# Retention values by token, retention gates kept in SBUF, and their units spread among the merge gates' in a one-core streaming layer on Trainium2

## The chip, the cores and the metric

The kernel runs on one core of one Trainium2 chip. The engines are PE (TensorE, matrix products; PEld is its weight load, which overlaps), DVE (VectorE), ACT (ScalarE), POOL (GpSimd, which here only issues stores) and SP (SyncE, which issues loads). Each works through its own queue in order and waits on semaphores for the others. The metric is the device time of one launch in microseconds (us), the median of several runs; lower is better.

## The reference, cut to what matters

One layer of a hybrid encoder for 512 prompt tokens and 8 x 16 sample tokens, so five token tiles of 128 (T = 640 columns). All is float32. The part that the change touches is the retention mixer, four heads with keys of 128 and values of 256:

```
h = rms_norm(x, norm_mix_g)
z = h @ w_in_mix                       # split into rq, rk, rv, rg, fq, fk, fv, ff, zg
q = rotary(rq); k = rotary(rk) * 128 ** -0.5; v = rv
per chunk: inter = (q @ state) * inter_decay
           intra = ((q @ k.T) * intra_decay) @ v
           state = state * chunk_decay + (k * kv_decay).T @ v
o_ret = rms_norm(inter + intra).reshape(B, S, 1024) * silu(rg)   # norm over the 256 values of a head
br_ret = o_ret @ w_br_ret
g = sigmoid(zg)                        # two merge gates of 1024 columns
y = (g[0] * br_ret + g[1] * br_fox) @ w_out
```

Two SwiGLU half steps, the forgetting attention (FoX) and a per-layer embedding stand around it and are not touched.

## The kernel before, in words

**Products.** Activations lie with channels on the partitions and tokens along the free axis. Each large matrix product is made of float32r pieces: ACT casts a weight block to `wh` (L281), DVE makes the rest `wl` (L282), and three matmuls of 320 columns are run per pair of blocks. Units of kind "s" of the mixer's projection use `MixSeven`, a Strassen-like scheme of seven products: `after(i)` combines the PSUM banks behind product i on ACT (L815 to L820) and DVE (L816 to L834). DVE's L830 and L833 are the last readers of the banks of a unit, and PE's next products need those banks. Behind them the two finished tiles of 128 x 640 (`z0`, `z1`) are stored by POOL to DRAM (`zdram`, 320 KB each; L831, L834).

**Order.** `run_units` is a generator over a list of units (`units`): it loads raw weights two units ahead on SP, splits them, runs products and yields. The attention and retention work is written by hand beside it: each step of a retention head is followed by `fill(FILL_R)`, which advances the generator by 2.45 us of PE work by a clock of the kernel's own. `until(("rg", hd))` would advance it until a head's gates exist. From this the framework's scheduler makes one fixed order for each engine, so a step that becomes shorter or longer moves what stands behind it by some instructions.

**List of units before.** FoX units, values `rv`, then "s" units of two tiles each: 2 for `rq`, 2 for `rk`, 4 for the retention gates `rg` (one per head), 8 for the merge gates, then two embedding units and four units of the FoX branch (`w_br_fox`). The heads run while the merge gates' units and those behind them are fed. The last merge unit also carries `embed_begin` and `fox_fetch`.

**A retention head.** `flip` turns the keys, `scores` makes `at` (scores times decay, keys on the partitions), `states_p` the running prompt states `behind`. `values(dvb)` makes, for each half of the value channels, a PSUM bank of 128 value channels x 512 prompt tokens out of seven float32 products of 128 columns, and ACT copies it to `o` (L1405). `square` squares both halves on ACT (L1421, L1423) and adds them on DVE (L1424). `values_s` makes the sample tile with tokens on the partitions and sums its squares on ACT with an accumulator (L1416, L1417). `sizes` sums the prompt's squares over the partitions with four matmuls of one column (out `pa`, in `ones`, `blk`), gathers them (L1431, L1432), and runs `rsqrt_mean` on DVE (L338 to L345: a chain of small operations); L1434 scales the sample tile. `gates` loads the head's two gate tiles back from `zdram` on SP and puts Silu on them (ACT, L1452). `states` makes the sample states and updates them with four DVE operations (L1478), which POOL stores. `finish` multiplies the gates on (L1463), spreads the token factors over the partitions with four matmuls (out `pa`, in `sm`, `ty`), multiplies with them (L1464), turns the sample tile with two transposes (L227) and gates it (L1465); POOL stores both tiles to `retd`, from where the `w_br_ret` products read them.

Silu (L1452) and the Sigmoid of the FoX branch (L1534) use different ACT function tables; a change between them shows as ACT_TABLE_LOAD.

Of the kernel before, what the change touches and what calls it, by code (L numbers as in the profile page):

```python
# [14 lines left out]
ALU = mybir.AluOpType  # L15
# [4 lines left out]
P = 128  # L20
# [25 lines left out]

FILL_P0, FILL_P1, FILL_S0, FILL_S, FILL_R, FILL_B = 1.76, 1.6, 19.8, 10.0, 2.45, 6.4
# [83 lines left out]
def kernel(  # L131
# [667 lines left out]

    class MixSeven(Seven):  # L800
# [9 lines left out]
        def after(self, i):  # L810
            a, b, c = (self.banks[k][:, :H2] if k in self.banks else None for k in "abc")
            r0, r1 = (mix_norm.rb[:, sl] for sl in HALVES)
            if i == 1:
                s1, self.w1 = tmp(), tmp()
                nc.scalar.copy(s1, a)  # L815
                nc.vector.tensor_tensor(b, b, s1, op=ALU.subtract)  # L816
                nc.scalar.copy(self.w1, b)
            elif i == 2:
                self.z1 = blk()
                nc.scalar.copy(self.z1[:, H2:], c)  # L820
                nc.vector.tensor_tensor(c, c, self.w1, op=ALU.subtract)
            elif i == 3:
                self.z0 = blk()
                nc.vector.tensor_tensor(self.z0[:, :H2], a, r0, op=ALU.mult)
            elif i == 4:
                s5 = self.z1[:, H2:]
                nc.vector.tensor_tensor(s5, b, s5, op=ALU.subtract)
                nc.vector.tensor_tensor(s5, s5, r1, op=ALU.mult)
            elif i == 5:
                nc.vector.tensor_tensor(self.z0[:, H2:], c, r1, op=ALU.mult)  # L830
                nc.gpsimd.dma_start(zdram[self.n0], self.z0)  # L831
            elif i == 6:
                nc.vector.tensor_tensor(self.z1[:, :H2], b, r0, op=ALU.mult)  # L833
                nc.gpsimd.dma_start(zdram[self.n0 + 1], self.z1)  # L834
# [489 lines left out]
    class Retention:  # L1324
# [70 lines left out]
        def values(self, dvb):  # L1395
            if dvb == 0:
                self.o = []
            dsl = slice(dvb * P, (dvb + 1) * P)
            po = bank()
            for t in range(4):  # L1400
                mm(po[:, t * P:(t + 1) * P], self.vs[t][:, dsl], self.at[:, t, :], True, t == 0, skip_group_check=True)
                if t > 0:
                    mm(po[:, t * P:(t + 1) * P], self.behind[t - 1][:, dsl], self.qd[:, t - 1, :], False, True, skip_group_check=True)
            o = blk()
            nc.scalar.copy(o[:, :S], po)  # L1405
            self.o.append(o)

        def values_s(self):
# [6 lines left out]
            self.os, sq, self.ms = tmp([P, DV]), tmp([P, DV]), tiny(1)  # L1415
            nc.scalar.copy(self.os, po[:, :DV])  # L1416
            nc.scalar.activation(sq, self.os, AF.Square, accum_out=self.ms)  # L1417

        def square(self):
            self.sq = blk([P, S])  # L1420
            nc.scalar.activation(self.sq, self.o[0][:, :S], AF.Square)  # L1421
            sq = blk([P, S])
            nc.scalar.activation(sq, self.o[1][:, :S], AF.Square)  # L1423
            nc.vector.tensor_tensor(self.sq, self.sq, sq, op=ALU.add)  # L1424

        def sizes(self):
            pm = bank()
            for t in range(4):
                mm(pm[:, t:t + 1], self.sq[:, t * P:(t + 1) * P], ones[:, 0:1], True, True)
            sums = tiny(TB)  # L1430
            nc.vector.tensor_copy(sums[:, :4], pm[:, :4])  # L1431
            nc.vector.tensor_copy(sums[:, 4:], self.ms)  # L1432
            self.ro = rsqrt_mean(sums, TB, 1.0 / DV)
            nc.vector.tensor_scalar(self.os, self.os, self.ro[:, 4:], None, op0=ALU.mult)  # L1434
# [12 lines left out]
        def gates(self):  # L1447
            self.g = []
            for dvb in range(2):
                g = blk()  # L1450
                load(g, zdram[Z_RG + 2 * self.hd + dvb])
                nc.scalar.activation(g, g, AF.Silu)  # L1452
                self.g.append(g)

        def finish(self):
            s0, pt = bank(), bank()
            for t in range(4):
                mm(s0[:, t * P:(t + 1) * P], self.ro[:, t:t + 1].to_broadcast([P, P]), ident, True, True)
# [113 lines left out]
    units += units_s(Z_G1, O_ZG + D, 8) + units_s(Z_G0, O_ZG, 8)  # L1572
    units[-1].begin, units[-1].middle = embed_begin, fox_fetch
# [69 lines left out]
    for hd, r in enumerate(heads):  # L1643
        for step in (
# [3 lines left out]
            lambda: r.values(0), lambda: (r.values(1), r.square()), lambda: r.values_s(),  # L1648
# [134 lines left out]
```

## Time and profile before

| what | value |
| --- | --- |
| median of 3 runs | 1646.37 us (1645.69 to 1647.33) |
| profiled execution: own time / span | 1648.36 us / 1646.6 us |
| PE busy, share of the span | 1631.5 us, 99% |
| DVE, ACT, POOL busy | 1165.6 us, 734.6 us, 98.9 us |
| granted TensorE clock, mean | 0.999 |
| retention heads in the trace | from about 880 to 1045 us |
| DMA | 248.15 MB, mean 151 GB/s |

The profile is that of one execution. Its time from launch to end is 1648.36 us, the span from the first to the last instruction 1646.6 us. The rows below carry, for each piece of work, its start in us from the start of the span, its length, the engine, the line and the operation with output and input names (buffer numbers left out); a bracket gives the idle time just before it on its engine and what ended it.

### The profile page before, as it was taken

The numbers are of one execution on the slowest core, as the hardware profiler recorded it, in microseconds if no ns is written. First come the engines' busy times: TensorE is split into PE (matmuls) and PEld (weight loads), VectorE is DVE, ScalarE is ACT, GpSimd is POOL, SyncE is SP. The second block draws the span as 40 slices with busy tenths as digits, with TensorE's granted clock in tenths as the row PEclk, the third lists the DMA queues.
The fourth block names the chain that finished last, engine by engine and source line by source line (L and its number), as shares of the span: only waits on it lengthen the run. The fifth ranks groups of instructions, "written<-read, shape, count | busy, mean of one in ns | idle before, by whom it ended". The sixth has DMA issues, their size and how long they took to land.

```text
span 1646.6 us, 30526 instructions
## 1 busy us (share of the span) xinstructions
PE 1631.5 (99%) x12067; PEld 1562.8 (95%) x12067; DVE 1165.6 (71%) x2476; ACT 734.6 (45%) x1516; POOL 98.9 (6%) x180
## 2 busy tenths in 40 slices
PE   9999999999999999999999899999999999999999
PEld 8999999999999888888799898999999999999998
DVE  7884786586876646766688895658885678568663
ACT  7552354244455444444434345435553355235432
POOL 0000000000111111000001111001000000000000
PEclk9999999999999999999999999999999999999999
DMA  7244223423623235566775576634333424432531
GB/s 245 77 143 141 93 87 124 150 85 108 210 81 117 90 111 170 219 257 229 279 255 195 194 262 242 228 109 161 95 116 134 134 77 132 136 117 88 172 120 46
DMA packets 207360, 248.15 MB, mean 151 GB/s; under 512 B 10432, under 2 KB 176240, under 8 KB 203120
## 3 DMA queue, kind: packets, MB, share of 16 engines
q1 hardware_dynamic: 194976, 202.69, 37.5%
q0 software_dynamic: 12032, 43.42, 6.7%
q8 instruction: 95, 1.56, 0.4%
q14 instruction: 49, 0.40, 0.1%
q10 hardware_dynamic: 208, 0.08, 0.0%
HBM read 197.51 MB, written 48.65 MB: 149 GB/s over the span
## 4 chain that ended last, share of the span: by engine, by line
PE 92%; DVE 3%; DMA 3%; ACT 1%; issue 1%; SPq 0%; DVEq 0%; ACTq 0%
PE pa L204 70%; PE pg L204 18%; PE pa L227 4%; DMA raw<-in_ffn_w_in_dram 2%; DVE wl L282 1%; DMA kv<-zdram 1%; DMA blk<-zdram 0%; ACT tmp L532 0%; ACT wh L281 0%; PE pg L227 0%; DVE raw L433 0%; DMA kv<-in_x_prompt_dram 0%; ACT blk L281 0%; ACT L1452 0%; DVE raw L422 0%
## 5 line engine op out<-in xcount | busy, mean ns | idle before, releaser
L281 ACT CAST wh<-raw 128x512 fp32r<-128x512 f32 (+1 forms) x525 | 315.5, 613 | 501.7 <-PE pa L204 319.7
L204 PE MATMUL pa<-blk,wh 128*128 128x320 f32 x2344 | 509.7, 310 | 2.8 <-ACT wh L281 1.0
L282 DVE TENSOR_TENSOR wl<-raw,wh 128x512 fp32r<-128x512 f32 (+1 forms) x525 | 351.4, 678 | 98.9 <-ACT wh L281 95.3
L204 PEld LDWEIGHTS pa<-blk,wh 128*128 128x128 f32 x2344 | 386.3, 188 | 10.9 <-ACT wh L281 2.8
L204 PE MATMUL pa<-blk,wl 128*128 128x320 f32 x1172 | 343.0, 308 | 0.0
L204 PE MATMUL pa<-kv,wh 128*128 128x320 f32 x1344 | 251.6, 308 | 0.0
L204 PEld LDWEIGHTS pa<-blk,wl 128*128 128x128 f32 x1172 | 215.4, 188 | 0.0
L204 PEld LDWEIGHTS pa<-kv,wh 128*128 128x128 f32 x1344 | 210.6, 188 | 0.0
L204 PE MATMUL pg<-blk,wh 128*128 128x320 f32 x768 | 177.0, 317 | 5.1 <-DVE blk L833 2.7
L204 PE MATMUL pa<-blk,blk 128*128 128x320 f32 (+2 forms) x1064 | 168.7, 304 | 0.0
L204 PE MATMUL pa<-kv,wl 128*128 128x320 f32 x672 | 154.5, 308 | 0.0
L204 PEld LDWEIGHTS pa<-blk,blk 128*128 128x128 f32 (+1 forms) x1064 | 151.9, 183 | 1.9 <-PE pa L204 1.2
L204 PE MATMUL pg<-wh,blk 128*128 128x256 f32 x768 | 148.0, 286 | 0.0
L204 PEld LDWEIGHTS pg<-blk,wh 128*128 128x128 f32 x768 | 127.4, 189 | 12.0 <-issue 5.8
L204 PEld LDWEIGHTS pg<-wh,blk 128*128 128x128 f32 x768 | 120.8, 188 | 6.8 <-issue 5.2
L204 PE MATMUL pg<-blk,wl 128*128 128x320 f32 x384 | 119.1, 310 | 0.0
L204 PEld LDWEIGHTS pa<-kv,wl 128*128 128x128 f32 x672 | 112.7, 188 | 0.0
L204 PE MATMUL pg<-wl,blk 128*128 128x256 f32 x384 | 108.4, 283 | 0.0
L282 DVE TENSOR_TENSOR blk<-raw,blk 128x512 fp32r<-128x512 f32 x82 | 56.2, 688 | 41.5 <-ACT blk L281 29.7
L204 PE MATMUL pa<-wh,blk 128*128 128x256 f32 (+1 forms) x432 | 82.3, 285 | 0.0
L281 ACT CAST blk<-raw 128x512 fp32r<-128x512 f32 x82 | 50.6, 621 | 61.1 <-DMA raw<-in_ffn_w_in_dram 47.8
L204 PEld LDWEIGHTS pg<-wl,blk 128*128 128x128 f32 x384 | 72.2, 188 | 1.6 <-issue 1.1
(293 smaller groups left out, 2250.1 us busy)
## 6 DMA issues: line engine op xcount, KB each, us to landing
raw<-in_ffn_w_in_dram SPq DMA_DIRECT2D x86, 512.0 KB, 4.7
raw<-in_w_in_mix_dram SPq DMA_DIRECT2D x25, 1024.0 KB, 5.7
raw<-in_ffn_w_out_dram SPq DMA_DIRECT2D x16, 1024.0 KB, 5.1
kv<-in_cache_fox_k_dram SPq DMA_DIRECT2D x16, 1024.0 KB, 6.3
kv<-in_cache_fox_v_dram SPq DMA_DIRECT2D x16, 1024.0 KB, 6.5
blk<-xd SPq DMA_DIRECT2D x48, 320.0 KB, 5.4
xd<-blk POOLq DMA_DIRECT2D x40, 320.0 KB, 2.4
zdram<-blk POOLq DMA_DIRECT2D x32, 320.0 KB, 3.4
```

What stands on the lines that cost most here:

```text
L204: i = nc.tensor.matmul(out, lhsT, rhs, start=start, stop=stop, **kw)
L227: tick(nc.tensor.transpose(out, in_, ident[: in_.shape[0], : in_.shape[0]]), 0.11)
L281: nc.scalar.copy(hi, src)
L282: nc.vector.tensor_tensor(lo, src, hi, op=ALU.subtract)
```

## The change

It has four parts.

1. **Values by token.** `values(u)` now makes two token tiles (128 tokens x 256 value channels) per bank: the scores or the scaled queries are the stationary operand and the values the moving one, so seven float32 products of 256 columns per head stand for fourteen of 128. ACT copies the bank (L1414) and squares each token tile with an accumulator (L1416), so that the sums of squares stand per token where `rsqrt_mean` needs them. The one-column matmuls, `square` and the gathering copies are gone.
2. **Scaling by token, then transposes.** `sizes` scales all five token tiles on DVE (L1434, 128 x 256 each). `finish` turns them with ten transposes (L228), and DVE multiplies the gates directly with the transposed bank (L1460) and the sample part (L1461). The four spreading matmuls and one 128 x 512 multiplication per half are gone.
3. **Gates kept.** The units of `rg` leave their tiles in SBUF (`kept`); their eight stores to and eight loads from `zdram` are gone.
4. **Order of units.** Five merge units come ahead of the first `rg` unit, one each ahead of the second and the third, none ahead of the fourth, and the last one behind it.

```diff
+MERGE_THEN = 5, 1, 1, 0
...
             elif i == 5:
                 nc.vector.tensor_tensor(self.z0[:, H2:], c, r1, op=ALU.mult)
-                nc.gpsimd.dma_start(zdram[self.n0], self.z0)
+                self.out(self.n0, self.z0)
...
+        def out(self, n, z):
+            if Z_RG <= n < Z_G1:
+                kept[n] = z
+            else:
+                nc.gpsimd.dma_start(zdram[n], z)
...
-        def values(self, dvb):
-            if dvb == 0:
-                self.o = []
-            dsl = slice(dvb * P, (dvb + 1) * P)
-            po = bank()
-            for t in range(4):
-                mm(po[:, t * P:(t + 1) * P], self.vs[t][:, dsl], self.at[:, t, :], True, t == 0, skip_group_check=True)
+        def values(self, u):
+
+            if u == 0:
+                self.o, self.ms = [], tiny(TB)
+            po, o, sq = bank(), att(shape=(P, 2, DV)), tmp([P, DV])
+            for n in range(2):
+                t, out = 2 * u + n, po[:, n * DV:(n + 1) * DV]
+                mm(out, self.at[:, t, :], self.vs[t], True, t == 0, skip_group_check=True)
                 if t > 0:
-                    mm(po[:, t * P:(t + 1) * P], self.behind[t - 1][:, dsl], self.qd[:, t - 1, :], False, True, skip_group_check=True)
-            o = blk()
-            nc.scalar.copy(o[:, :S], po)
-            self.o.append(o)
+                    mm(out, self.qd[:, t - 1, :], self.behind[t - 1], False, True, skip_group_check=True)
+            nc.scalar.copy(o.rearrange("p n v -> p (n v)"), po)
+            for n in range(2):
+                nc.scalar.activation(sq, o[:, n, :], AF.Square, accum_out=self.ms[:, 2 * u + n:2 * u + n + 1])
+                self.o.append(o[:, n, :])
...
         def sizes(self):
-            pm = bank()
-            for t in range(4):
-                mm(pm[:, t:t + 1], self.sq[:, t * P:(t + 1) * P], ones[:, 0:1], True, True)
...
+            ro = rsqrt_mean(self.ms, TB, 1.0 / DV)
+            for t, o in enumerate(self.o):
+                nc.vector.tensor_scalar(o, o, ro[:, t:t + 1], None, op0=ALU.mult)
...
-                g = blk()
-                load(g, zdram[Z_RG + 2 * self.hd + dvb])
+                g = kept.pop(Z_RG + 2 * self.hd + dvb)
                 nc.scalar.activation(g, g, AF.Silu)
...
         def finish(self):
-            s0, pt = bank(), bank()
-            for t in range(4):
-                mm(s0[:, t * P:(t + 1) * P], self.ro[:, t:t + 1].to_broadcast([P, P]), ident, True, True)
+            pts, pt = [bank(), bank()], bank()
             for dvb in range(2):
-                transpose(pt[:, dvb * P:(dvb + 1) * P], self.os[:, dvb * P:(dvb + 1) * P])
-            for dvb in range(2):
-                o, g = self.o[dvb], self.g[dvb]
-                nc.vector.tensor_tensor(o[:, :S], o[:, :S], g[:, :S], op=ALU.mult)
-                nc.vector.tensor_tensor(o[:, :S], o[:, :S], s0, op=ALU.mult)
-                nc.vector.tensor_tensor(o[:, S:], g[:, S:], pt[:, dvb * P:(dvb + 1) * P], op=ALU.mult)
-                nc.gpsimd.dma_start(retd[2 * self.hd + dvb], o)
+                for t, o in enumerate(self.o):
+                    transpose(pts[dvb][:, t * P:(t + 1) * P] if t < 4 else pt[:, dvb * P:(dvb + 1) * P], o[:, dvb * P:(dvb + 1) * P])
+            for dvb, g in enumerate(self.g):
+                nc.vector.tensor_tensor(g[:, :S], g[:, :S], pts[dvb], op=ALU.mult)
+                nc.vector.tensor_tensor(g[:, S:], g[:, S:], pt[:, dvb * P:(dvb + 1) * P], op=ALU.mult)
+                nc.gpsimd.dma_start(retd[2 * self.hd + dvb], g)
...
-    for hd in range(RH):
+    merge = units_s(Z_G1, O_ZG + D, 8) + units_s(Z_G0, O_ZG, 8)
+    merge[-1].begin, merge[-1].middle = embed_begin, fox_fetch
+    for hd, n in enumerate(MERGE_THEN):
+        units += [merge.pop(0) for _ in range(n)]
         units += units_s(Z_RG + 2 * hd, O_RG + hd * DV, 2)
...
+    units += merge
```

PE's instructions have the same order and shapes before and after up to the first head's values (the units that changed places are alike), and again from the `w_br_ret` products on. Three places in between follow. Lines of the changed kernel lie 1 to 4 off those of the one before (L1474 and L1478 are the same state update).

On PE, at the end of the first head before: the four spreading matmuls (in `sm`, `ty`) and two transposes stand behind a unit's product, and the turning of the next head's keys (in `sm`, `kv`) follows.

```order
L204 MATMUL pa_10851<-blk_5104,wl_10831 128x320
L204 MATMUL pa_10909<-sm,ty_10807 128x128 x4
L227 MATMUL pa_10910<-sm,tmp_10767 128x128 x2
L227 MATMUL pa_11019<-sm,kv_10515 128x128 x4
L227 MATMUL pa_11020<-sm,kv_10515 128x128
```

The same place on PE after: ten transposes of the scaled token tiles (`att`, and `tmp` for the samples) stand there.

```order
L205 MATMUL pa_10835<-blk_5044,wl_10716 128x320
L228 MATMUL pa_10893<-sm,att_10674 128x128 x2
L228 MATMUL pa_10893<-sm,att_10706 128x128 x2
L228 MATMUL pa_10895<-sm,tmp_10760 128x128
L228 MATMUL pa_10894<-sm,att_10674 128x128 x2
L228 MATMUL pa_10894<-sm,att_10706 128x128 x2
L228 MATMUL pa_10895<-sm,tmp_10760 128x128
L228 MATMUL pa_11004<-sm,kv_10515 128x128 x4
```

What moved: before, PE needed from DVE the factors `ty` alone; now it needs five scaled tiles. Between the product that fills bank `pg_10665` and these transposes PE has 30 product matmuls and three of the states' (128 x 256) to run. On DVE after, ahead of those transposes, from the last bank reader L833 (of `pg_10665`) on:

```order
L833 TENSOR_TENSOR blk_10703<-pg_10665,blk_5485 128x320
L345 SCALAR_TENSOR_TENSOR ty_10792<-ty_10792,ty_10790 128x5
L1474 SCALAR_TENSOR_TENSOR kv_10358<-kv_10358,pa_10843 128x512
L283 TENSOR_TENSOR wl_10815<-raw_10429,wh_10814 128x512
L346 SCALAR_TENSOR_TENSOR ty_10791<-ty_10792,ty_10791 128x5
L1474 SCALAR_TENSOR_TENSOR kv_10358<-kv_10358,pa_10844 128x512
L1474 SCALAR_TENSOR_TENSOR kv_10358<-kv_10358,pa_10845 128x512
L434 TENSOR_TENSOR raw_10429<-raw_10429 128x4x128
L1434 TENSOR_SCALAR att_10674<-att_10674,ty_10791 128x256 x2
L1434 TENSOR_SCALAR att_10706<-att_10706,ty_10791 128x256 x2
L1434 TENSOR_SCALAR tmp_10760<-tmp_10760,ty_10791 128x256
```

What moved: before, one scaling (the sample tile) stood behind the four state updates; now five do, and the two multiplications with the gates that stood ahead of the state updates stand behind the transposes.

On ACT, in the last head before, Silu (L1452) and Sigmoid (L1534) alternate, each with a table load:

```order
L1416 COPY tmp_12378<-pa_12368 128x256
L1452 ACT_TABLE_LOAD
L1452 ACTIVATE blk_12427<-blk_12427 128x640
L1417 ACTIVATE tmp_12379,ty_12380<-tmp_12378 128x256
L1534 ACT_TABLE_LOAD
L1534 ACTIVATE blk_12124<-blk_12124 128x640
L1452 ACT_TABLE_LOAD
L1452 ACTIVATE blk_12430<-blk_12430 128x640
```

After, all eight Silus stand ahead of the first Sigmoid (now L1530), and the last head's stretch on ACT reads:

```order
L1530 ACT_TABLE_LOAD
L1530 ACTIVATE blk_11905<-blk_11905 128x640
L1507 COPY tmp_11983<-pg_11976 128x256
L1530 ACTIVATE blk_11907<-blk_11907 128x640
L282 CAST wh_12242<-raw_12079 128x512
L1414 COPY att_12256<-pa_12255 128x512
L304 CAST blk_12417<-blk_12415 128x640
L1416 ACTIVATE tmp_12257,ty_12254<-att_12256 128x256 x2
L1530 ACTIVATE blk_11988<-blk_11988 128x640
```

What moved: six table loads in the retention stretch become two.

## Rows read from the trace of the kernel before

**Rows 1.** The page's busy times with their shares of the span, and the chain of work that ended last by engine.

```profile
PE 1631.5 (99%) x12067; PEld 1562.8 (95%) x12067; DVE 1165.6 (71%) x2476; ACT 734.6 (45%) x1516; POOL 98.9 (6%) x180
PE 92%; DVE 3%; DMA 3%; ACT 1%; issue 1%; SPq 0%; DVEq 0%; ACTq 0%
```

**Rows 2.** Busy time by stretch: length, then PE, PEld, DVE, ACT, POOL with their counts, the granted clock, the DMA share and GB/s.

```profile
880.00:940.00 60.00, 58.05 (x413) 53.59 (x412) 51.54 (x117) 24.04 (x46) 6.32 (x11) 1.00 0.60 195
944.00:948.00 4.00, 4.00 (x21) 4.00 (x20) 2.02 (x5) 0.94 (x2) 0.25 (x1) 0.57 0.94 327
```

**Rows 3.** All waits of PE from 880 to 1045 us: engine, tile and line that waited, what ended the wait, us in total, times, longest.

```profile
PE pg L204 <- DVE blk L833: 2.7, 2, 2.3
PE pg L204 <- DVE blk L1541: 1.2, 1, 1.2
PE pg L204 <- DVE blk L830: 1.2, 1, 1.2
PE pa L204 <- DVE att L1390: 0.4, 1, 0.4
```

**Rows 4.** PE in order of time: start, length, operation and count. A float32 matmul shows as two of the count.

```profile
893.49 1.05 PE L204 MATMUL pa<-sm,ty 128*128 128x128 f32 x8
894.38 0.38 PE L227 MATMUL pa<-sm,tmp 128*128 128x128 f32 x2
894.59 0.71 PE L227 MATMUL pa<-sm,kv 128*128 128x128 f32 x5
907.23 0.59 PE L204 MATMUL pa<-kv,att 128*128 128x256 f32 x2
907.66 0.61 PE L204 MATMUL pa<-att,kv 128*128 128x128 f32 x4
915.01 0.60 PE L204 MATMUL pa<-att,kv 128*128 128x128 f32 x4
915.45 0.61 PE L204 MATMUL pa<-att,att 128*128 128x128 f32 x4
931.49 0.95 PE L204 MATMUL pa<-ones,blk 128*128 128x1 f32 x8
932.30 0.54 PE L204 MATMUL pg<-blk,wh 128*128 128x320 f32 x2
```

**Rows 5.** PE in order of time around its longest wait, in the second head.

```profile
943.13 0.53 PE L204 MATMUL pg<-blk,wh 128*128 128x320 f32 x2 [2.31 <-DVE blk L833]
943.64 0.45 PE L204 MATMUL pg<-blk,wh 128*128 128x320 f32 x2
944.07 0.72 PE L204 MATMUL pg<-blk,wh 128*128 128x320 f32 x2
945.65 1.91 PE L204 MATMUL pa<-sm,ty 128*128 128x128 f32 x8
947.36 0.45 PE L227 MATMUL pa<-sm,tmp 128*128 128x128 f32 x2
```

**Rows 6.** The chain that ended last, pieces in order of time (start, length, what), ahead of that wait.

```profile
928.29 6.70 DMA blk<-zdram
935.07 0.75 ACT blk L1452
935.84 0.69 DVE blk L1463
939.44 1.20 DVE kv L1478 x2
```

**Rows 7.** DVE in order of time at the same place.

```profile
935.84 0.69 DVE L1463 TENSOR_TENSOR blk<-blk,blk 128x512 f32<-128x512 f32 x1 [1.67 <-ACT blk L1452]
942.50 0.48 DVE L833 TENSOR_TENSOR blk<-pg,blk 128x320 f32<-128x320 f32 x1
```

**Rows 8.** The chain that ended last in the fourth head, ahead of PE's wait for L1541.

```profile
1018.75 1.28 ACT L1452
1020.05 0.75 ACT blk L1452
1020.82 0.69 DVE blk L1463
```

**Rows 9.** Groups of instructions of DVE and ACT from 800 to 1060 us by line and shape: count, busy us, mean ns of one, idle time before them.

```profile
L1464 DVE TENSOR_TENSOR blk<-blk,pa 128x512 f32<-128x512 f32 x8 | 5.1, 680 | 0.6 <-PE pa L204 0.6
L1424 DVE TENSOR_TENSOR blk<-blk,blk 128x512 f32<-128x512 f32 x4 | 2.7, 683 | 0.8 <-ACT blk L1423 0.8
L1434 DVE TENSOR_SCALAR tmp<-tmp,ty 128x256 f32<-128x256 f32 x4 | 1.4, 346 | 0.0
L1452 ACT ACT_TABLE_LOAD x3 | 3.8, 1283 | 0.2 <-DMA blk<-zdram 0.2
L1421 ACT ACTIVATE blk<-blk 128x512 f32<-128x512 f32 x4 | 2.6, 639 | 0.0
L1417 ACT ACTIVATE tmp<-tmp 128x256 f32<-128x256 f32 x4 | 1.6, 409 | 0.0
L1417 ACT ACTIVATION_READ_ACCUMULATOR tmp<-tmp 128x1 f32 x4 | 0.7, 187 | 0.0
```

**Rows 10.** Waits of DVE for the next heads' queries and keys, 880 to 1045 us.

```profile
DVE kv L1353 <- DMA kv<-zdram: 2.9, 1, 2.9
DVE kv L1352 <- DMA kv<-zdram: 2.1, 1, 2.1
```

More of the change, by code (lines that the diff above doesn't have):

```diff
@@ L798, in split @@
                 self.w[i] = split_w(self.raw[:, :, i * P:(i + 1) * P] if self.kind == "t" else self.raw[:, i * ks:(i + 1) * ks, :])
+    kept = {}
     class MixSeven(Seven):
@@ L830, in after @@
                 nc.vector.tensor_tensor(self.z0[:, H2:], c, r1, op=ALU.mult)
-                nc.gpsimd.dma_start(zdram[self.n0], self.z0)
+                self.out(self.n0, self.z0)
             elif i == 6:
                 nc.vector.tensor_tensor(self.z1[:, :H2], b, r0, op=ALU.mult)
-                nc.gpsimd.dma_start(zdram[self.n0 + 1], self.z1)
+                self.out(self.n0 + 1, self.z1)
+        def out(self, n, z):
[3 more added lines that the diff above has]
+                nc.gpsimd.dma_start(zdram[n], z)
     def run_units(units):
@@ L1414, in values_s @@
                     mm(po[pr * 32:(pr + 1) * 32, :DV], self.qg[:, pr, j, :], self.st[:, 2 * pr + j, :], False, j == 1, skip_group_check=True)
[L1415 to L1424, printed above, removed]
-        def sizes(self):
-            pm = bank()
-            for t in range(4):
-                mm(pm[:, t:t + 1], self.sq[:, t * P:(t + 1) * P], ones[:, 0:1], True, True)
[L1430 to L1434, printed above, removed]
+            o, sq = tmp([P, DV]), tmp([P, DV])
+            nc.scalar.copy(o, po[:, :DV])
+            nc.scalar.activation(sq, o, AF.Square, accum_out=self.ms[:, 4:])
+            self.o.append(o)
+        def sizes(self):
+            ro = rsqrt_mean(self.ms, TB, 1.0 / DV)
+            for t, o in enumerate(self.o):
+                nc.vector.tensor_scalar(o, o, ro[:, t:t + 1], None, op0=ALU.mult)
         def flip(self):
@@ L1568 @@
     units[-1].done = lambda: ready.add("rk")
-    for hd in range(RH):
+    merge = units_s(Z_G1, O_ZG + D, 8) + units_s(Z_G0, O_ZG, 8)
+    merge[-1].begin, merge[-1].middle = embed_begin, fox_fetch
+    for hd, n in enumerate(MERGE_THEN):
+        units += [merge.pop(0) for _ in range(n)]
         units += units_s(Z_RG + 2 * hd, O_RG + hd * DV, 2)
         units[-1].done = lambda hd=hd: ready.add(("rg", hd))
-    units += units_s(Z_G1, O_ZG + D, 8) + units_s(Z_G0, O_ZG, 8)
-    units[-1].begin, units[-1].middle = embed_begin, fox_fetch
+    units += merge
     units += [Unit("n", w_ple[0][:, q * 256:(q + 1) * 256], embed_take(q), x=p_x) for q in range(2)]
@@ L1647 @@
             lambda: (r.states_p(), heads[hd + 1].loads() if hd + 1 < RH else None),
-            lambda: r.values(0), lambda: (r.values(1), r.square()), lambda: r.values_s(),
+            lambda: r.values(0), lambda: r.values(1), lambda: r.values_s(),
             lambda: (r.sizes(), until(("rg", hd)), r.gates()),
```

## The prediction

> **What bounds the kernel now.** I read the page's busy times first, then the chain, then PE's waits, and only then single stretches. PE is busy 1631.5 us of 1646.6, and 92% of the chain that ended last is PE [rows 1]. So the kernel gets faster in two ways only: less PE work, or fewer of the few places where PE stands. The reader is to see that a saved microsecond on ACT (45%) or DVE (71%) counts only if PE was waiting for it. In the heads' stretch DVE is much fuller than on average: 51.54 us of 60, or 86%, from 880 to 940 us [rows 2]. There a wait of DVE is caught up slowly.
>
> PE's waits between 880 and 1045 us are all for DVE: 2.7 + 1.2 + 1.2 + 0.4 = 5.5 us in five places [rows 3]. The longest, 2.31 us, is in the second head. Behind it the clock falls: 944 to 948 us shows a granted mean of 0.57 [rows 2], that is, mostly the 1.2 GHz level, after an idle PE.
>
> **Part 1, PE's work.** Prices are distances between starts, since matmuls overlap.
> - Removed: the one-column matmuls of a head take 932.30 - 931.49 = 0.81 us [rows 4]; four heads, 3.24.
> - Removed: the four spreading matmuls take 894.38 - 893.49 = 0.89 [rows 4]; four heads, 3.56.
> - Added: 8 more transposes per head. Two take 894.59 - 894.38 = 0.21, so 0.105 each [rows 4]; 32 of them, 3.36.
> - Exchanged: a 128-column float32 product costs 0.44 / 2 = 0.22 (915.01 to 915.45), a 256-column one 0.43 (907.23 to 907.66) [rows 4]. 56 x 0.22 = 12.32 become 28 x 0.43 = 12.04: 0.28 less.
> - Returning from a float32 piece to the split products costs a little: the first pair takes 0.54 instead of 0.45 [rows 4, 5]. In the order of instructions such pieces number 86 before and 78 after: 8 x 0.09 = 0.7 less. Bounds 0 to 0.7.
>
> Sum: -3.24 - 3.56 + 3.36 - 0.28 - 0.7 = **-4.4 us** (-3.7 without the returns). All of it lies on PE, so on the path.
>
> The added transposes have a price that can be disputed: the row says 0.105 us, with the granted clock at 1.00 over that whole stretch [rows 2, 4]. The Trainium skill, "TensorE: Matmul & The Clock Gate", Part 4 on PE-mode transpose, gives about 275 ns for a 128x128 transpose in one kernel and says that transposes don't count as PE-busy for the clock in the same way. By its duration the 32 would cost an estimated 8.8 us and the sum of this part would be +1.0; the trace does not agree with the duration. What its second statement would do here is weighed among the rivals.
>
> **Part 2, the wait in the second head.** The chain shows its cause: a gate load (6.70 us from 928.29), Silu on ACT at 935.07, then DVE's L1463 at 935.84 [rows 6], which had left DVE idle for 1.67 us [rows 7]. Behind it stand two state updates at 0.60 each from 939.44 [rows 6], two more, and only then L833, 942.50 to 942.98 [rows 7]; PE, which needs its bank, starts at 943.13 after 2.31 us [rows 5]. With the gates kept, the load and the wait go, and by the new order both L1463 (0.60 each, like their neighbours of the same size) stand behind the transposes: 1.67 + 1.20 = 2.87 us less ahead of L833, more than the 2.31. The state updates still stand ahead of it, and DVE has little slack. So I take 1.9 of the 2.31 as gone; bounds 0 and 2.3. **-1.9 us.**
>
> If PE no longer stands there for long, the clock shouldn't fall. Cost of the fall: six product matmuls from 944.07 to 945.65 take 1.58 where three took 0.43 just before (943.64 to 944.07), 0.72 too much; the spreading matmuls take 1.71 (945.65 to 947.36) [rows 5] where 0.89 is usual [rows 4], 0.82 too much. **-1.5 us**, bounds 0 and 1.5.
>
> **Part 3, the tables.** Six table loads of 1283 ns in this stretch [rows 9] become two. ACT gains 4 x 1.28 = 5.1 us, and pays for accumulating squares: per head four of 409 + 187 ns for two of 639 [rows 9], 2.38 - 1.28 = 1.1, so 4.4 over four heads. ACT breaks even, and it isn't the bound. The loads reach PE in one place: in the fourth head a load at 1018.75, Silu at 1020.05 and L1463 at 1020.82 hold DVE [rows 8], and L1541 behind it lets PE wait 1.2 us [rows 3]. That Silu is now done early. **-1.2 us**, bounds 0 and 1.2.
>
> **Part 4, the new wait.** The transposes wait for DVE's scalings, in order behind everything queued there. Neither exists before, so I count both sides from the moment at which the bank of L833 is full in the first head. DVE has, by the new order, L833 (0.40 to the next start, as an operation of 0.48 [rows 7] lets the next begin some 0.08 early, compare 0.60 [rows 6] with 0.68 [rows 9]), three state updates, one weight rest and one combination (five of 0.60), two chain steps (0.08 each) and five scalings of 0.346 [rows 9], so 0.27 apart: 0.40 + 3.0 + 0.16 + 1.35 = 4.9, with some 0.2 for the hand-over 5.1. PE has 30 product matmuls (0.43 / 3 = 0.144 each [rows 5], 4.3) and three of 256 columns (1.3), with a return 5.7. PE would come 0.6 us too late to wait, if DVE starts on time. It often doesn't: its five waits here mean 5.5 / 5 = 1.1 us late [rows 3]. I take 1.1 - 0.6 = 0.5; bounds 0 and 2.3 - 0.6 = 1.7. In the second head the same count has PE and DVE within some 0.3 us of each other: 0.3, bounds 0 and 2.0. In the third, two of the four state updates now stand behind the scalings, and in the fourth PE has 37 matmuls in between: 0, bounds 0 and 1 each. **+0.8 us.** Queued behind the scalings on DVE are L836, which frees a bank, and weight rests; PE would wait for those next.
>
> **Part 5, the rest.** DVE loses the 5.1 of L1464 and 2.7 of L1424 and gains 16 x 0.346 = 5.5 [rows 9]: 2.3 us less, cover rather than gain. Sixteen transfers of 320 KB go from POOL's and SP's queues. DVE's two waits for the next heads' data (2.9 and 2.1 [rows 10]) give PE the waits for L830, for L1390 and the short one for L833, 2.0 us together [rows 3]. Those loads wait for a buffer that the state's store must leave first; that store now comes some microseconds earlier, but raw weights still queue ahead on SP. I take 0, bounds -2.0 (all go) and +2.0. Kept gates hold up to eight tiles longer; no PE wait for such a tile is in the rows: 0, up to 1.
>
> **Sum.** -4.4 - 1.9 - 1.5 - 1.2 + 0.8 = **-8.2 us**. Against the profiled execution's own 1648.36 that is 1640.2; that execution lies 2.0 above the median of 1646.37, so against the median **1638.2 us**, 0.50% less.
>
> **Rivals.**
> - *All stalls go, none comes*: DVE is on time at every scaling, and the earlier state store removes the waits for data. -4.4 - 2.3 - 1.5 - 1.2 - 2.0 = -11.4: 1635.0. For it: a whole DVE idle of 1.67 goes and the queues have less to do. Against: DVE at 86%.
> - *The lateness only moves*: what PE no longer waits for at L833 it waits for at the transposes. In the first and second head 2.3 us each, the largest wait seen, and the clock falls after one: -8.2 - 0.8 + 4.6 + 1.5 = -2.9: 1643.5; with waits for data 2.0 longer, 1645.5. Or PE doesn't stand, but the runs of transposes themselves let the clock fall in each of four heads: -8.2 + 4 x 1.5 = -2.2: 1644.2. The skill's sentence on transposes in the place named above would make that so. Against this: seven transposes in a row at 894.38 leave the clock at 1.00 [rows 2, 4]; ten with the next head's five are not in the trace.
> - *Slower*: DVE, still behind by four state updates, reaches the scalings far behind PE in three heads. Each wait w brings the fall of 1.5. The gains are 9.0; slower by more than 3.3 needs 3 x (w + 1.5) > 12.3, so w > 2.6 us in each. With 3.0: -9.0 + 13.5 = +4.5, 1650.9. For it: the transposes need five scalings more than the factors alone, behind the same updates. Against: no wait so far was over 2.31, and the counts of part 4 lie near zero.
> - *It doesn't do what it says in the second head*: the state updates, not the gate load, made L833 late. The 2.31 and the fall stay: -8.2 + 1.9 + 1.5 = -4.8: 1641.6. It lies within the forecast's own range.
>
> **How the numbers follow.** A measurement of this kernel can tell about 0.2%, 3.3 us, so faster is below 1643.1 and slower above 1649.7. Forecast (1636.5 to 1642) 0.47; all stalls go (1633 to 1636.5) 0.18; the lateness moves (1643.1 to 1648) 0.25; slower (around 1651) 0.10. Faster 0.65, same 0.25, slower 0.10. The range reaches from the lower end of the second case to most of the third: 1633 to 1647.5; it leaves out the slower case and some of the rest.
>
> **What would show it.** No row of `ones` or of `ty` products and PE's wait for L833 below 0.5 us: parts 1 and 2. Transposes about 0.1 us apart with the clock at 1.00: part 1 against the skill's rule. Two table loads, none ahead of the last head's products: part 3. PE's waits for L1434 below 1 us in all: part 4; 2 us or more in two heads, with a clock below 1.00 behind them, would make the prediction wrong, as would longer waits of DVE for `kv` loads.

## The result, and the profile after

The changed kernel takes 1637.53 us (median of 6 runs, 1636.49 to 1638.45), the kernel before 1646.40 in the same comparison: ratio 0.9945, 95% interval 0.9933 to 0.9957, so 9.1 us less (7.1 to 11.0). A second comparison gave 0.9942 (0.9928 to 0.9956). Here and below, medians and ratios leave out four single executions that took 1971 us or more, far longer than the others of their kernel.

The page's busy times and the chain by engine of the changed kernel, which answer to [rows 1]; its own time was 1636.49, its span 1634.5:

```profile
PE 1624.8 (99%) x11979; PEld 1555.4 (95%) x11979; DVE 1164.5 (71%) x2472; ACT 733.1 (45%) x1536; POOL 94.5 (6%) x172
PE 97%; ACT 1%; DVE 1%; DMA 1%; issue 0%; SPq 0%; DVEq 0%
```

PE has 6.7 us less busy time, and its share of the chain that ended last rises from 92 to 97%: waits have left the chain as well as work.

All waits of PE from 880 to 1045 us, where the kernel before had five [rows 3]:

```profile
PE pg L205 <- DVE blk L833: 1.1, 1, 1.1
```

PE in order of time at that wait and at the transposes behind it (start, length, operation, count), and the windows around it (length, busy PE, PEld, DVE, ACT, POOL, granted clock, DMA share, GB/s), which answer to [rows 5] and [rows 2]:

```profile
933.50 0.53 PE L205 MATMUL pg<-blk,wh 128*128 128x320 f32 x2 [1.10 <-DVE blk L833]
937.07 0.60 PE L228 MATMUL pa<-sm,att 128*128 128x128 f32 x4
937.51 0.27 PE L228 MATMUL pa<-sm,tmp 128*128 128x128 f32 x1
937.62 0.60 PE L228 MATMUL pa<-sm,att 128*128 128x128 f32 x4
938.05 0.27 PE L228 MATMUL pa<-sm,tmp 128*128 128x128 f32 x1
```

```profile
920.00:940.00 20.00, 18.90 (x136) 17.61 (x136) 19.39 (x50) 8.65 (x18) 1.98 (x3) 1.00 0.63 218
940.00:960.00 20.00, 20.00 (x138) 19.55 (x137) 20.00 (x44) 9.23 (x23) 1.08 (x2) 1.00 0.60 204
```

The wait in the second head is 1.10 us where it was 2.31, and the clock stays at 1.00 behind it. Four transposes take 0.44 (937.07 to 937.51), 0.11 each; none of this head's waits for its scaled tile. The last of the five scalings ends at 936.34. DVE is busy 19.39 of 20 us there, where the kernel before has 17.53 from 920 to 940 us.

DVE in order of time at the same place (the bracket: idle time and what ended it), which answers to [rows 7] and [rows 10]:

```profile
915.64 0.83 DVE L1362 TENSOR_TENSOR kv<-kv,blk 128x640 f32<-128x640 f32 x1 [2.26 <-DMA kv<-zdram]
932.87 0.48 DVE L833 TENSOR_TENSOR blk<-pg,blk 128x320 f32<-128x320 f32 x1
```

In the order of time, what remains of PE's wait begins with DVE's 2.26 us for the next head's queries: the only idle time that DVE's rows show from there to L833 is 0.23 us at 922.57, so it never catches up. Whether that load alone sets the wait is taken up among the experiments.

Groups of instructions from 800 to 1060 us (count, busy us, mean ns), which answer to [rows 9]:

```profile
L1434 DVE TENSOR_SCALAR att<-att,ty 128x256 f32<-128x256 f32 x16 | 5.0, 376 | 0.0
L1416 ACT ACTIVATE tmp<-att 128x256 f32<-128x256 f32 x16 | 6.7, 418 | 0.1
L1451 ACT ACT_TABLE_LOAD x1 | 1.3, 1283 | 0.0
L1530 ACT ACT_TABLE_LOAD x1 | 1.3, 1283 | 0.0
L228 PE MATMUL pa<-sm,att 128*128 128x128 f32 x48 | 7.1, 273 | 0.0
```

Two table loads are left of six. The mean length of a transpose is 273 ns, its distance to the next 0.11 us: the records of successive transposes overlap, so the distance is what one more costs.

**Where the time went.** PE's instructions have the same order of shapes up to 862 us and again from the `w_br_ret` products on. In between the kernel before takes 187.2 us (862.5 to 1049.7), the changed one 176.7 (862.0 to 1038.7): 10.5 less. A second profiled execution of the changed kernel (its repetition below) takes 176.7 there too. Summing each shape's distances to the next start there, with the waits of [rows 3] and the slow clock of [rows 5] taken out, gives:

| term | forecast us | in the traces us |
| --- | --- | --- |
| one-column matmuls gone | -3.2 | -3.3 |
| spreading matmuls gone | -3.6 | -3.6 |
| transposes added | +3.4 | +3.5 |
| values in 256 columns, returns to split products | -1.0 | -1.4 |
| wait in the second head (2.31 to 1.10) | -1.9 | -1.2 |
| fall of the clock | -1.5 | -1.5 |
| wait in the fourth head | -1.2 | -1.2 |
| transposes waiting for scalings | +0.8 | 0 listed (0.2 hidden in the row of the transposes) |
| waits that start with the next heads' data | 0 | -2.0 |
| sum | -8.2 | -10.7 |

The 0.2 us stand in the first head: the transpose of the sample tile starts at 887.76, 0.32 behind the one ahead of it where 0.11 is usual, and its scaling ends at 887.61. The view of waits doesn't list it.

The two profiled executions differ by 11.9 us in their own time, 3 more than the medians: that of the kernel before lies 2.0 above its median, that of the changed one 1.0 below. Their spans differ by 12.1 us, of which 1.6 lie outside the heads. The medians decide the size of the total, the traces its parts.

### The profile page after: what moved, and what is told of

Same layout as the page of the kernel before. It is cut to its first block, busy times and chain, and to the rows that moved or that the text cites. A ratio compares the mean times of both kernels' runs of the same rounds, so it can differ in the third digit from the quotient of the medians.

```text
span 1634.5 us, 30303 instructions
## 1 busy us (share of the span) xinstructions
PE 1624.8 (99%) x11979; PEld 1555.4 (95%) x11979; DVE 1164.5 (71%) x2472; ACT 733.1 (45%) x1536; POOL 94.5 (6%) x172
## 4 chain that ended last, share of the span: by engine, by line
PE 97%; ACT 1%; DVE 1%; DMA 1%; issue 0%; SPq 0%; DVEq 0%
PE pa L205 74%; PE pg L205 19%; PE pa L228 4%; ACT tmp L533 0%; DMA raw<-in_ffn_w_in_dram 0%; PE pg L228 0%; ACT wh L282 0%; DMA kv<-in_x_prompt_dram 0%; DVE kv L1474 0%; ACT blk L361 0%; DVE wl L283 0%; DVE raw L424 0%; DVE tmp L573 0%; ACT blk L353 0%; DVE raw L420 0%
```

## The experiments

**The parts alone.** Four kernels hold one or two parts of the change. The diffs are those above, cut:

```diff
# values only                     # gates and order: before, with
 MERGE_THEN  (not used)           +MERGE_THEN = 5, 1, 1, 0
+def values(self, u): ...         +self.out(self.n0, self.z0)
+def finish(self): ...            +g = kept.pop(Z_RG + 2 * self.hd + dvb)
 load(g, zdram[...])
# order only: before, with        # values and order: changed kernel, with
+MERGE_THEN = 5, 1, 1, 0          -g = kept.pop(...)
                                  +g = blk(); load(g, zdram[...])
```

> The kernel before with the values by token, the scaling and the transposes alone; gates go through DRAM and the units stand in the old order. Theory A (the sum of parts: the PE work of this part is worth 4.4 to 4.8 us wherever the gates lie, and the waits belong to the gates and to DVE's load): 1640 to 1642.5 us, PE's products as in the changed kernel, the waits in the heads partly left. Rival B (the gates on chip carry the gain, the values none): 1645 to 1647. Rival C (the values alone give all of it, since the multiplication with the gates moves behind the transposes): 1637 to 1639.

> The kernel before with the gates kept in SBUF and the new order of units; values, sizes and finish as before. Theory A: only waits and the fall of the clock go, 2 to 5 us: 1641.5 to 1644.5, with the 16 one-column and 16 spreading matmuls still there and DVE no longer idle for Silu in the second head. Rival B: 1637 to 1639. Rival C: 1645.5 to 1647.

> The kernel before with the new order of units alone; the gates still go through DRAM. Theory A: the loads of the gates now lie closer behind their stores, so nothing is gained and up to 4 us are lost: 1645.5 to 1650. Rival D (the order is what removes the waits, keeping the gates adds nothing): 1641.5 to 1644.5, like the run with gates kept.

> The changed kernel with the gates through DRAM (stored by POOL, loaded by SP) instead of kept. Theory A: PE's work as in the changed kernel, a wait for the gates' loads on ACT, which reaches PE only through the last multiplications: 1638 to 1642. If keeping the gates is worth nothing in the new order (rival D): 1637 to 1638.5.

| kernel | median us | ratio to before | 95% interval |
| --- | --- | --- | --- |
| before (same chip) | 1647.66 | 1 | |
| order only | 1647.08 | 0.9994 | 0.9986 to 1.0003 |
| gates and order | 1647.33 | 0.9997 | 0.9989 to 1.0006 |
| values only | 1641.20 | 0.9960 | 0.9947 to 0.9972 |
| values and order | 1641.69 | 0.9966 | 0.9953 to 0.9978 |
| all (two comparisons of their own) | 1637.53, 1638.19 | 0.9945, 0.9942 | 0.9928 to 0.9957 |

The order alone does nothing that can be measured; rival D falls. All of PE's waits in its heads (860 to 1050 us) are those of the kernel before, to a tenth, but for the shortest:

```profile
PE pg L206 <- DVE blk L835: 2.6, 2, 2.3
PE pg L206 <- DVE blk L1543: 1.2, 1, 1.2
PE pg L206 <- DVE blk L832: 1.2, 1, 1.2
```

The values are worth about 5.6 to 6.6 us by themselves (4 to 9 by the intervals), which fits PE's work of 4.7; rival B falls. Keeping the gates is worth another 3.5 to 4 us (0.9966 against 0.9945 and 0.9942; the intervals overlap a little, but the slowest run of the changed kernel, 1638.71, lies below the fastest of values and order, 1640.73), but only on top of the values: without them it is worth nothing that can be measured. No theory had both. Theory A said 1641.5 to 1644.5 for gates and order, which take 1647.33; rival C was nearest there (1645.5 to 1647), but said 1637 to 1639 for the values only, which take 1641.20. So the parts don't add up, and the next question is where the gates' gain goes.

*Values only*: the four longest of PE's waits in the heads, then ACT, DVE and PE in order of time in the second head, and a window behind it.

```profile
PE pg L205 <- DVE ty L346: 2.0, 1, 2.0
PE pg L205 <- DVE blk L830: 1.7, 1, 1.7
PE pg L205 <- DVE blk L1535: 1.0, 1, 1.0
PE pa L228 <- DVE att L1431: 0.9, 2, 0.7
```

```profile
932.51 0.74 ACT L1449 ACTIVATE blk<-blk 128x640 f32<-128x640 f32 x1 [4.33 <-DMA blk<-zdram]
933.79 0.69 DVE L283 TENSOR_TENSOR wl<-raw,wh 128x512 fp32r<-128x512 f32 x1 [2.66 <-ACT wh L282]
934.93 0.56 PE L205 MATMUL pg<-blk,wh 128*128 128x320 f32 x2 [1.67 <-DVE blk L830]
938.97 0.87 PE L205 MATMUL pg<-blk,wh 128*128 128x320 f32 x2 [2.01 <-DVE ty L346]
```

```profile
940.00:942.00 2.00, 2.00 (x9) 2.00 (x8) 2.00 (x7) 0.00 (x0) 0.81 (x2) 0.50 0.91 369
```

Here the multiplication with the gates already stands behind the transposes, as the prediction had it, and yet a gate load still stops PE, by another way: Silu waits 4.33 us for the load, a weight cast stands behind it in ACT's queue, DVE's `wl` waits 2.66 for the cast, and L830 and L833 come late behind `wl`, with the four state updates between them. PE stands 1.67 and 2.01 us (the second row names L346, a short step right behind L833; both end within 0.15 us ahead of PE's start), and the clock falls to the 1.2 GHz level (0.50). So for the wait to go, the load has to go; moving L1463 was not enough. The 0.9 us for L1431 is the forecast's new wait of transposes for scalings: it exists in this kernel.

*Gates and order*: the four longest of PE's waits in the heads.

```profile
PE pa L206 <- DVE blk L1434: 1.9, 1, 1.9
PE pa L229 <- DMA tmp<-in_p_prompt_dram: 1.7, 1, 1.7
PE pg L206 <- DVE ty L346: 1.1, 1, 1.1
PE pa L206 <- DVE ty L347: 0.6, 2, 0.3
```

The third of them stands in the second head, where the kernel before waits 2.31 us:

```profile
942.49 0.54 PE L206 MATMUL pg<-blk,wh 128*128 128x320 f32 x2 [1.07 <-DVE ty L346]
```

The load is gone, and with it the fall of the clock: the windows from 880 to 1050 us show 1.00. In the second head the wait has shrunk to 1.07 us (L346 again ends right behind the reader of the bank, L837 here, L833 before), as in the changed kernel, although both multiplications with the gates still stand ahead of that reader (928.25 and 930.59). But other waits have come: the one-column matmuls wait 1.9 us for the sum of squares, which DVE adds behind other work (L1424 before, here L1434), the spreading matmuls for the last steps of the root, and the embedding's transposes 1.7 for a load that stands on SP behind one that waits for a state's store. With 0.4 and 0.4 more they are 6.1 us, where the kernel before has 5.5.

**The changed kernel again, and three edits of it.**

> The changed kernel once more, so that it stands on the same chip as the three that follow. From the first comparison: a ratio of 0.9945 to the kernel before.

1638.19 us, 0.9942; the same single wait of 1.1 us for L833.

Transposes twice:

```diff
-                for t, o in enumerate(self.o):
+                for t, o in [(t, o) for t, o in enumerate(self.o) for _ in range(2)]:
                     transpose(pts[dvb]...)
```

> The changed kernel with each of the ten transposes of a head run twice in a row (the same output; 40 more in all). Theory A (0.105 us each by the rows, the clock stays): 4.2 us more than the changed kernel, the granted clock at 1.00 behind them. Rival E (the rule of the Trainium skill, TensorE: Matmul & The Clock Gate, Part 4: a transpose takes about 275 ns and does not keep the clock up): an estimated 11 us more, or the clock falls behind the longer runs, 1.5 us each in up to four heads, 6 us on top of the 4.2.

1639.66 us, ratio 0.9951 (0.9938 to 0.9964): 1.5 more than the changed kernel. On PE the 40 additional transposes take 4.1 us by their distances, 0.103 each, as theory A says. The time grows by less because more than the transposes has moved: the order of PE and DVE differs from the changed kernel's from 888 us on. PE's waits fall from 1.1 to 0.3 us, and its other shapes take 1.8 us less by their distances. In the second head PE arrives about a microsecond later, and L833 (931.63) now stands ahead of the scalings and of all four state updates (from 933.35); PE doesn't wait for it, although DVE waits 2.6 us for the queries, 2.3 in the changed kernel. Windows over two runs of twenty transposes, and PE's only wait from 880 to 1045 us:

```profile
880.00:900.00 20.00, 20.00 (x145) 19.02 (x144) 19.93 (x48) 6.48 (x14) 3.08 (x5) 1.00 0.75 269
930.00:950.00 20.00, 20.00 (x150) 19.45 (x149) 18.76 (x45) 7.02 (x13) 1.99 (x3) 1.00 0.73 232
```

```profile
PE pg L205 <- DVE blk L1537: 0.3, 1, 0.3
```

The clock stays at 1.00. Rival E falls in this kernel. The Trainium skill (TensorE: Matmul & The Clock Gate, Part 4) gives about 275 ns for a transpose. The trace agrees with that as the length of one (273 in the rows after), not as what one costs in a run of them.

Scaling on ACT:

```diff
-                nc.vector.tensor_scalar(o, o, ro[:, t:t + 1], None, op0=ALU.mult)
+                nc.scalar.activation(o, o, AF.Copy, scale=ro[:, t:t + 1])
```

> The changed kernel with the twenty scalings by token on ACT instead of DVE. Theory A (DVE, 97% busy ahead of PE's last wait in the second head, is what sets that wait): DVE loses 1.4 us of work per head, the wait of 1.1 us for L833 shrinks only if the scalings stand ahead of it; 0 to 1 us less. Rival F (ACT's queue, with the weight casts behind the scalings, becomes the wait): 0 to 3 us more, PE waiting for wh casts.

1637.62 us, 0.9940 (0.9927 to 0.9953): no difference to the changed kernel. The wait for L833 stays at 1.1: the scalings stand behind L833 on DVE, so their place doesn't reach it. PE waits for no cast more. Rival F falls.

Queries apart:

```diff
+            self.wq = w = blk()          # in first_loads
+            load(w[:half, :], zdram[Z_RQ + hd, half:, :], 40.0)
+            load(w[half:, :], zdram[Z_RQ + hd, :half, :], 40.0)
...
-            load(b[:half, :T], zdram[Z_RQ + hd, half:, :], 40.0)
-            load(b[half:, :T], zdram[Z_RQ + hd, :half, :], 40.0)
-            self.z = [(a[:, 0, :], a[:, 1, :]), (a[:, 2, :], b[:, :T])]
+            self.z = [(a[:, 0, :], a[:, 1, :]), (a[:, 2, :], self.wq)]
```

> The changed kernel with the half-swapped queries of a head in a tile of their own, loaded with the head's first loads, instead of in the tile that holds the values, whose buffer comes free only when the head before has used its queries. Theory A (DVE's 2.3 us wait for that load at 915 us is what makes L833 late and PE wait 1.1 us): the wait for L1362 goes, PE's 1.1 us goes, 0.5 to 1.1 us less than the changed kernel. Rival G (four state updates ahead of L833 alone make it late): PE still waits about 1 us there, no change.

1641.30 us, 0.9964 (0.9951 to 0.9977): 3 us slower than the changed kernel, which neither theory said. DVE's waits for data, then PE's waits in the heads:

```profile
DVE blk L1363 <- DMA blk<-zdram: 4.6, 2, 3.8
DVE kv L1362 <- DMA kv<-zdram: 2.0, 1, 2.0
```

```profile
PE pg L205 <- DVE blk L833: 1.6, 1, 1.6
PE pa L205 <- DVE blk L1461: 1.0, 1, 1.0
PE pg L205 <- DVE blk L1538: 0.9, 1, 0.9
PE pg L205 <- ACT tmp L820: 0.6, 1, 0.6
```

DVE waits longer for the queries in their new place than in the old, and other waits follow. PE's 1.6 us for L833 stands at 904.19, straight behind DVE's wait of 3.8 for the queries (to 902.31); in the second head L833 no longer holds PE. The edit moved the wait instead of removing it, and the orders of the engines with it (from 851 us on), so it couldn't tell theory A from rival G.

**The remaining wait, and the gates without the values.**

Queries not loaded (the rotation of the queries reads the keys' half-swapped tile, so the retention's scores are other numbers):

```diff
-            load(b[:half, :T], zdram[Z_RQ + hd, half:, :], 40.0)
-            load(b[half:, :T], zdram[Z_RQ + hd, :half, :], 40.0)
-            self.z = [(a[:, 0, :], a[:, 1, :]), (a[:, 2, :], b[:, :T])]
+            self.z = [(a[:, 0, :], a[:, 1, :]), (a[:, 2, :], a[:, 1, :])]
```

> The changed kernel without the loads of the half-swapped queries: their rotation reads the tile of the half-swapped keys instead, so the prompt's and sample's scores are other numbers; every operation of DVE and PE stays. Theory A (DVE's wait of 2.3 us for that load sets PE's last wait of 1.1 us): no wait for L1362 in the second head, no wait of PE for L833, 0.5 to 1.5 us less than the changed kernel: 1636.5 to 1637.7 where that one has 1638.2. Rival G (the four state updates ahead of L833 set it): the wait of PE stays at about 1 us.

1640.19 us, 0.9957 (0.9944 to 0.9970). All waits of PE in the heads:

```profile
PE pa L205 <- DMA kv<-in_state_ret_dram: 2.8, 1, 2.8
PE pg L205 <- ACT tmp L820: 0.2, 1, 0.2
```

The wait for L833 is gone, although the four state updates still stand ahead of it. DVE is no longer behind there, as theory A says: it waits for PE instead, 0.85 us at one of those updates and 1.33 at L819 (923.94).

```profile
921.92 0.69 DVE L1472 SCALAR_TENSOR_TENSOR kv<-kv,pa 128x512 f32<-128x512 f32 x1 [0.85 <-PE pa L205]
932.93 0.49 DVE L833 TENSOR_TENSOR blk<-pg,blk 128x320 f32<-128x320 f32 x1
```

But this is no proof. PE's and DVE's orders differ from the changed kernel's from 851 us on, and one of the four updates now stands 11 us ahead of L833. The execution runs 1.06 us later than that of the changed kernel already ahead of the heads; with that taken off, L833 comes 1.0 us earlier, and PE reaches the same product 0.6 later. So the run speaks for late queries as part of the cause, and rival G isn't excluded: in the run with the transposes twice the queries come as late, the updates stand behind L833, and PE doesn't wait either.

The time is about 2 us more than the changed kernel's all the same, and the waits account for it: 2.85 and 0.25 us where there was 1.1. The last head's state lands about as before (17.2 us behind its issue, 16.5 in the changed kernel again), but in the new order PE asks for it at 991.6 instead of 997.4 us. The forecast of the total was wrong for that reason.

Half sum (in the kernel with gates and order alone, the norm is over half the values):

```diff
             sq = blk([P, S])
             nc.scalar.activation(sq, self.o[1][:, :S], AF.Square)
-            nc.vector.tensor_tensor(self.sq, self.sq, sq, op=ALU.add)
```

> The kernel before with gates kept and the new order, as in the run that showed no gain, but the one-column matmuls read the squares of the first half of the values only: DVE's addition of the two halves is left out, and so the norm is over half the values. Theory H (keeping the gates gave nothing there because PE's one-column matmuls now wait for that addition, 1.9 us in the first head): this wait goes, 1.5 to 3 us less than that run: 1644.5 to 1646. Rival I (DVE is full in any case, so the wait turns up at its next reader): no more than the 2.7 us of DVE work in four additions is felt nowhere, 1646.5 to 1647.5.

1645.98 us, 0.9992 (0.9983 to 1.0001): 0.8 us less than gates and order by the ratios, between the two and not clear of the noise (the intervals overlap). The 1.9 us of the one-column matmuls is gone. In its place PE waits 0.9 and 1.2 us at the same time (891.65 and 894.83) for ACT's copies of a unit's banks:

```profile
PE pa L229 <- DMA tmp<-in_p_prompt_dram: 1.8, 1, 1.8
PE pg L206 <- ACT tmp L821: 1.2, 1, 1.2
PE pa L206 <- ACT tmp L819: 0.9, 1, 0.9
PE pg L206 <- DVE ty L346: 0.6, 1, 0.6
```

So theory H is right about the wait and wrong about its price; rival I's picture, the wait turning up at the next reader, is the nearer one, though at ACT and not DVE.

Finish first (the last two steps of a head exchanged in the changed kernel):

```diff
-            lambda: (r.states(), heads[hd + 1].more_loads() if hd + 1 < RH else None), lambda: r.finish(),
+            lambda: r.finish(), lambda: (r.states(), heads[hd + 1].more_loads() if hd + 1 < RH else None),
```

> The changed kernel with a head's last two steps exchanged: the transposes and the multiplication with the gates stand ahead of the sample states, so that the scalings and L833 stand ahead of the four state updates on DVE. Theory A with rival G (the updates ahead of L833 hold PE): PE's 1.1 us for L833 goes, 0.5 to 1.1 us less. Against it: the state's store comes later and so do the next heads' loads; if these set the time, 1 to 3 us more, DVE waiting longer for kv loads.

1645.58 us, 0.9991 (0.9983 to 1.0000): about 8 us slower than the changed kernel. L833 holds PE no longer, but three waits for ACT's copies come, and the clock falls again: 0.91 from 960 to 980 us and 0.83 from 980 to 1000. The two longest begin with weight loads: ACT's cast waits for the weights (0.3 us in all in the changed kernel), and the copy (L820 at 961.15, L1507 at 985.16) stands behind the cast.

```profile
PE pg L205 <- ACT tmp L1507: 3.0, 1, 3.0
PE pg L205 <- ACT tmp L820: 2.4, 1, 2.4
PE pa L205 <- ACT tmp L818: 1.5, 1, 1.5
```

```profile
960.62 0.62 ACT L282 CAST wh<-raw 128x512 fp32r<-128x512 f32 x1 [2.92 <-DMA raw<-in_w_ple_dram]
984.64 0.62 ACT L282 CAST wh<-raw 128x512 fp32r<-128x512 f32 x1 [5.92 <-DMA raw<-in_w_br_fox_dram]
```

```profile
960.00:980.00 20.00, 18.38 (x125) 17.00 (x126) 15.24 (x43) 12.16 (x33) 4.39 (x8) 0.91 0.85 281
980.00:1000.00 20.00, 16.96 (x99) 15.09 (x97) 11.08 (x22) 7.13 (x13) 4.67 (x8) 0.83 0.91 324
```

Nearly the whole gain of the change is eaten by an exchange of two steps, and not over the loads of `kv` that were expected: DVE waits 2.9 us for those, 3.9 in the changed kernel. Why these weights weren't there in time was not tested. No version tried is measurably faster than the changed kernel.

## Why the prediction was right, and where it wasn't

It said 1638.2 us, and 1637.53 was measured; where the forecast has -8.2, the comparison shows -9.1 (-7.1 to -11.0). Point by point:

- **Part 1, PE's work: right.** -4.4 forecast, -4.7 in the traces; the values alone measured 5.6 to 6.6 with the waits left about as they were (6.0 us where the kernel before has 5.5). The smaller part was split wrongly: the 256-column products saved 1.4 instead of 0.3, the returns nothing instead of 0.7. The price of a transpose is 0.103 to 0.11 us by the distances on PE, shown by doubling them. That the trace does not agree with a duration of about 275 ns, as the prediction had it, holds for this price alone: as a length the rows show 273.
- **Part 2, the wait in the second head: the gate load right, the size off.** The prediction added 1.67 us of waiting for the gate and 1.20 for the two moved L1463 to 2.87 less ahead of L833, and took 1.9 of the 2.31; 1.2 came. The term for L1463 doesn't show: in gates and order, where the load is gone and L1463 still stands ahead, PE waits 1.07 us there, in the changed kernel 1.10; in values only, where L1463 is moved and the load stays, it waits 1.67 and 2.01, through Silu, the weight cast and `wl`. What is left begins, in the order of time, with the next head's queries, which the prediction had priced apart at nothing; that they alone cause it isn't shown. Its own sign, less than 0.5 us for L833, did not come. The clock's 1.5 us came as forecast: with 1.1 us of idle PE it did not fall.
- **Part 3, the tables: right** for the changed kernel, -1.2: six loads became two, and the wait for L1541 is gone. That the tables did it isn't shown. The kernels of the parts fit: with six loads of tables (order only) PE waits 1.2 us there, with four (values only, values and order) 1.0, with two (gates and order, the changed kernel) not at all. But with two loads as well, "queries apart" has 0.9 us for the same line and "transposes twice" 0.3, and no run changed the tables alone.
- **Part 4, the new wait: too dear.** +0.8 forecast, 0.2 measured, in the first head. There the count had PE 0.6 us behind DVE; in the trace the fifth scaled tile comes 0.2 too late for PE. The addition of an average lateness was the larger error. The wait is real in the kernel with the values alone (0.9 us).
- **Part 5, the next heads' data: mis-sized.** 0 taken, -2.0 in the traces, the end of its bound. The three waits of PE that began there went; DVE's own waits fell only from 5.0 to 3.9 us. In values only the three are gone too, with the same 3.9 us of DVE's waits, so kept gates aren't needed for it; what did it wasn't tested further.

By the table the errors don't cancel: 0.7 us less than forecast in part 2 stand against 0.3 more in part 1, 0.8 in part 4 and 2.0 in part 5, and the heads got 10.5 us shorter where 8.2 was said. That the median lies within 0.7 us of the forecast is in part luck: the profiled execution before, from which the waits were read, lay 2.0 us above its median. In the waits, the rival "all stalls go" came nearest: one of five is left, by half.

What stays open: why keeping the gates gives 3.5 to 4 us with the values and nothing without. PE's waits account for the sizes. Without the values they grow from 5.0 us (order only) to 6.1 (gates and order), which takes back most of what the fall of the clock had cost, some 1.5; with the values they shrink from 5.2 (values and order) to 1.1, and the fall goes too. Why the other waits come in the one kernel and not in the other isn't shown. The one attempt to remove the largest gave 0.8 us of it back (the intervals of the two runs overlap), and the 1.7 us for the embedding's load was not tried separately. Keeping the gates in the old order of units was not tried either, so what the order is worth once the gates are kept isn't known. And each edit of the changed kernel moved the order of the engines, from 851 to 888 us on, and not only at its own place, so none of them changed one wait alone.

## What to carry to other kernels

Work taken off an engine that is busy 99% is a gain that can be counted from rows, by distances between starts; here it came with and without the other parts. A wait that is removed is worth only what the next waiter in the same in-order queues doesn't take: look through the queue of each engine that the late data passes (here ACT's casts behind Silu, DVE's rests behind the casts), not only at the instruction that shows the wait. And an exchange of two steps can cost as much as a good change gains, so order and work should be measured apart. An edit that is to remove one wait must leave the order of the other instructions alone, or it can't tell which wait mattered: compare the order of both traces before reading the time.

## What the runs showed of the hardware that had not been expected

A transpose of 128x128 in float32 shows 273 ns of length and takes 0.103 to 0.11 us in a row; twenty of them in a row left the granted clock at 1.00. The clock fell behind PE's idle times of 1.67 and 2.01 us with 2 us of products between them (values only, 0.50 behind them), of 2.31 alone (before, 0.57 over 4 us), and of 2.41 and 3.04 (finish first, 0.91 and 0.83 over 20 us each). It stayed at 1.00 behind 1.10 alone, and also behind 2.85 alone in the kernel without the queries' loads (1.00 from 994 to 1002 us): so the length of the one wait doesn't decide it, and what does was not tested. The Trainium skill, "TensorE: Matmul & The Clock Gate", Part 4, says that transposes do not count as PE-busy for the clock in the same way; ten or twenty between products, some 1 and 2 us, did not show it here.
